# Later first seven-product pair, evenly spaced forms of x, and whole k blocks in the opening four products of a decoder step

## Chip, cores and metric

The kernel runs on one NeuronCore of a Trainium2 chip. The metric is the device time of one launch in microseconds (us), as the median over several runs.

## What is computed

One decoder layer for 264 tokens (256 of a new sequence, 8 of samples), all in float32 at the interface. Width is 2048, the inner width of each feed-forward block is 5504.

```python
def swiglu(x, wg, wu, wd):
    return (jax.nn.silu(x @ wg) * (x @ wu)) @ wd
...
        h = h + 0.5 * swiglu(rmsnorm(h, norm_ffn1[l]), ffn1_gate[l].astype(jnp.float32),
                             ffn1_up[l].astype(jnp.float32), ffn1_down[l].astype(jnp.float32))
        mix, C_f, n_f, m_f, buf = mixing_block(...)
        h = h + mix
        h = h + 0.5 * swiglu(rmsnorm(h, norm_ffn2[l]), ...)
    y = rmsnorm(h, norm_final).astype(x.dtype)
```

The change touches only the two `swiglu` parts, called layer "1" and layer "2" in the code (ffn of the first and of the second half-step).

## The kernel before, in words

**Numbers.** Every float32 weight and activation is cut into two float16 parts, hi and lo. A product of a 128x128 weight block with 264 columns of x is then three matmuls: hi with hi, hi with lo, lo with hi. The loads bring a raw float32 tile `wraw` of up to eight blocks (`fetch`, DMA issued by SP at L240); ScalarE writes `whi` (`high`, L219); VectorE writes `wlo` (`low`, L227). Six buffers of each exist and about five tiles are kept ahead (`AHEAD`). Each engine works strictly in the order in which the program emits its instructions; there is no scheduler, so the order is the one in which the Python code runs.

**Layer 1's opening.** `products4` (matmuls at L504) computes gate and up of blocks 0 and 1 together, in parts of k listed in the table `FIRST`, while x itself arrives block by block (`ahead`, DMA at L858) and is cut into its parts. Then blocks 2 and on follow as ordinary products (`product` with `three`, L286 to L288): 16 k blocks, 48 matmuls, in two tiles of eight k blocks ("chunks"). After gate of a block: product with the norm's factor, Silu; after up: product with the gate and a cut into hi and lo for the down projection. The norm's sum of squares (`square_pairs`, ScalarE L687 and VectorE L691) is formed beside this and summed over partitions by a matmul at L622 (`column_sums`), after which the outputs of blocks 0 to 2 are taken from PSUM in one go.

**Blocks by seven products.** For the blocks in `SEVEN`, gate and up are formed together as a 2x2 by 2x2 block product with seven instead of eight products, in two parts (`chunk_by_seven`, L408, c = 0 beside block j and c = 1 two blocks later): 168 matmuls of 132 columns instead of 96 of 264. This needs sums of weights, made in `prepare` (raw loads `sraw` issued by GpSimd at L330; `sa` and `sb` parts by ScalarE and VectorE; `ssum` by VectorE at L354 to L356), in eight numbered steps, one step per chunk of an ordinary product (`prepare_step`). It also needs eight forms of x (`form`: two ScalarE scalings at L658 and three GpSimd operations at L662 to L664; `form_split`: a ScalarE cut, and half a product later a VectorE cut `f` at L227). The forms use GpSimd (`side`).

**When.** `at(delta, ...)` puts a function on an agenda delta products ahead; `tick` counts a product at its start (steps of 1) and between its two chunks (0.5). The forms of x run from block 3 on (gate of block 3 is product 1), the last cut 6.5 products on. The raw loads of the first pair stand in the program just before block 3; since GpSimd has nothing ahead of them that waits, nothing in its queue holds them back in layer 1. `lag` delays each VectorE cut of weights by one tile, from block 3 on.

Of the kernel before, what the change touches and what calls it, by code (L numbers as in the profile page):

```python
# [8 lines left out]
F32 = mybir.dt.float32  # L9
# [11 lines left out]
NFB = DFF // 128  # L21
# [20 lines left out]

BRANCHING = [getattr(mybir.EngineType, e) for e in ("SP", "Activation", "PE", "DVE")]

FIRST = [(0, 1, 0, 2), (1, 1, 0, 2), (0, 1, 2, 2), (1, 1, 2, 2), (2, 1, 0, 4), (3, 1, 0, 4)]
FIRST += [(k, 2, j, 2) for k in range(4, KB, 2) for j in (0, 2)]

SEVEN = list(range(7, 22, 3)) + list(range(22, NFB, 3))  # L50
TH = T // 2


# [25 lines left out]
    return {"h": head_blocks, "c": conv_blocks, "o": lambda ob: [O + ob]}[item[0]](n)  # L79


def weight_plan(a, apart=()):


    plan = []

    def add(key, src, n, m=128):
        parts = -(-n // WK)
        cut = [n * i // parts for i in range(parts + 1)]
        for k0, k1 in zip(cut, cut[1:]):  # L90
            plan.append((key, src[:, k0:k1, :], k1 - k0, m, 1))

    def ffn(layer, first):
        gu, d = a[f"w{layer}gu"], a[f"w{layer}d"]
        for half, blocks in enumerate(HALVES):
            for j in blocks:
                if j >= first and j not in apart:
                    add((layer, "g", j), gu[j, 0], KB)
                    add((layer, "u", j), gu[j, 1], KB)
            for db in range(KB):  # L100
                b0, b1 = blocks[0], blocks[-1] + 1
                add((layer, "d", half, db), d[db][:, b0:b1, :], b1 - b0)

    four = a["w1gu"][0:2].rearrange("j g p k m -> p (j g) k m")
    for k0, nk, j0, nj in FIRST:
        plan.append(("four", four[:, j0 : j0 + nj, k0 : k0 + nk, :], nj * nk, 128, nj))
    ffn("1", 2)
    add("gates", a["wg"], KB, 64)
    for item in MIX_ORDER:
        for b in mix_blocks(item):  # L110
            add(("in", b), a["win"][b], KB)
    half = KB // 2
    for k0 in (0, half):
        for db in range(2):
            add(("out", db), a["wout"][db][:, k0 : k0 + half], half)
    for db in range(2, KB):
        add(("out", db), a["wout"][db], KB)
    ffn("2", 0)
    return plan

# [24 lines left out]
def step(ctx: ExitStack, tc: tile.TileContext, a: dict, shared, bad=None):  # L145
# [64 lines left out]

    plan = weight_plan(a, SEVEN if half_size else ())
    ready = []

    def high(dst, src, scale=1.0):
# [99 lines left out]
    def prepare(pool, layer):  # L316

        gu = a[f"w{layer}gu"]  # L320
        ks = [slice(0, 4), slice(4, 8)]
        raws = [None, None]
        steps.clear()
        step_no[0] = None

        def load(j, c):
            raws[c] = raw = pool.tile([128, 4, 4, 128], F32, tag="raw", name="sraw", bufs=2)
            for g in range(2):
                blocks = gu[j, g].rearrange("p (s k) m -> p s k m", s=2)
                queue.dma_start(raw[:, 2 * g : 2 * g + 2], blocks[:, :, ks[c], :])  # L330

        def blocks(j, c):
            if c == 0:
                formed[j, 0] = [
                    pool.tile([128, 3, 8, 128], PART, tag=f"sa{i}", name=f"sa{i}")
                    for i in range(2)
                ]
            high(formed[j, 0][0][:, :, ks[c]], raws[c][:, 0:3], sw)

        def blocks_low(j, c):  # L340
            hi, lo = formed[j, 0]
            low(lo[:, :, ks[c]], raws[c][:, 0:3], hi[:, :, ks[c]], sw)

        sums = [None]

        def all_sums(j, c):
            raw = raws[c]
            if c == 0:
                formed[j, 1] = [
                    pool.tile([128, 4, 8, 128], PART, tag=f"sb{i}", name=f"sb{i}")  # L350
                    for i in range(2)
                ]
            sums[0] = s = pool.tile([128, 4, 4, 128], F32, tag="ssum", name="ssum")
            nc.vector.tensor_tensor(s[:, 2], raw[:, 2], raw[:, 3], op=ALU.add)  # L354
            nc.vector.tensor_tensor(s[:, 3], s[:, 2], raw[:, 1], op=ALU.subtract)
            nc.vector.tensor_tensor(  # L356
                s[:, 0:2], raw[:, 0:4:2],
                s[:, 3].unsqueeze(1).to_broadcast([128, 2, 4, 128]), op=ALU.subtract,
            )
            high(formed[j, 1][0][:, :, ks[c]], s, sw)  # L360

        def sums_low(j, c):
            hi, lo = formed[j, 1]
            low(lo[:, :, ks[c]], sums[0], hi[:, :, ks[c]], sw)

        for n, j in enumerate(SEVEN):
            for s, fn, c in (
                (2, blocks, 0), (3, blocks_low, 0), (3, blocks, 1), (4, blocks_low, 1),
                (5, all_sums, 0), (6, sums_low, 0), (7, all_sums, 1), (8, sums_low, 1),
            ):  # L370
                steps.setdefault(8 * n + s - (3 if n == 0 else 0), []).append((fn, j, c))
            for c in range(2):
                s = -4 if n == 0 else 8 * n + (-2, -1)[c]
                steps.setdefault(s, []).append((load, j, c))
# [148 lines left out]
    if half_size:  # L523
        stat = const.tile([128, NSTAT], F32, name="stat")
        nc.gpsimd.memset(stat, 2.0 * SUMS[0])
        squares = const.tile([128, 6], F32, name="squares")
        twins = const.tile([128, 2, 2 * len(SEVEN)], F32, name="twins")
        twin = iter(range(2 * len(SEVEN)))

    def watch(ps, rows=None):  # L530

# [186 lines left out]
    def ffn(layer, norm, done, start=None, end=None):  # L718
        with ExitStack() as stack:
# [2 lines left out]
                tc.tile_pool(name=f"forms_{norm.tag}", bufs=1)  # L722
            )
            early = {}

            def gate_up(j, which):
                return early.pop((j, which), None) or product((layer, which, j), norm.x, range(KB))
# [47 lines left out]
                prepare(spool, layer)  # L775
            for half, blocks in enumerate(HALVES):
                act = {}
                step_end[0] = 8 * len(SEVEN) + 8

                order = []  # L780
                for i, j in enumerate(blocks):
                    if half_size and j in SEVEN:
                        order += [("seven", i, j, 0)]
                    elif half_size and j - 2 in SEVEN:
                        order += [("seven", i - 2, j - 2, 1), ("one", i, j, 0)]
                    else:
                        order += [("one", i, j, 0)]
                for kind, i, j, c in order:
                    if kind == "seven":
                        if c == 0:  # L790
                            seven[j] = [bank() for _ in range(3)]
                        chunk_by_seven(j, c, norm.x, norm.forms, seven[j])
                        if c == 1:
                            by_seven(j, i)
                        continue
                    if first and start is not None:

                        ps4 = start()
                        for n, ps in enumerate(ps4):
                            early[n // 2, "gu"[n % 2]] = ps  # L800
                        for step, pairs in ((0, (0, 1, 2)), (1, (3, 4)), (1.5, (5, 6)), (2, (7,))):
                            at(step, norm.square_pairs, fpool, pairs)
                        tick(0)
                        for which in "gu":
                            early[2, which] = product((layer, which, 2), norm.x, range(KB))
                    if half_size and j == 3:
                        for k in range(8):
                            if k:
                                at((1.5, 2.5, 3, 4, 4.5, 5.5, 6)[k - 1], norm.form_split, k - 1)
                            at((1, 1.5, 2.5, 3, 4, 4.5, 5.5, 6)[k], norm.form, k)  # L810
                        at(6.5, norm.form_split, 7)
                        for fn, *what in steps.pop(-4):
                            fn(*what)
                    if half_size and j == SEVEN[0] - 3:
                        step_no[0] = -4
                    if half_size and half == 0 and j == blocks[-1]:

                        step_end[0] = step_no[0]
                    lag[0] = half_size and j >= 3
                    pg = gate_up(j, "g")  # L820
                    if first:
                        norm.finish()
                        first = False
                    zg = t264("ta")
                    nc.vector.tensor_tensor(zg, pg, norm.r, op=ALU.mult)
                    watch(pg)
                    sg = t264("tb")
                    nc.scalar.activation(sg, zg, AF.Silu)
                    pu = gate_up(j, "u")
                    zu = t264("tc")  # L830
                    nc.vector.tensor_tensor(zu, pu, norm.r, op=ALU.mult)
                    activated(j, i, zu, sg)
                    watch(pu)
# [827 lines left out]
```

## Time and profile before

| | before |
|---|---|
| median of 3 runs | 1831.66 us (1831.6 to 1832.43) |
| profiled execution, its own time | 1831.9 us |
| its span | 1830.2 us |
| TensorE (PE) busy | 1799.4 us, 98% |
| VectorE (DVE) busy | 1400.8 us, 77% |
| ScalarE (ACT) busy | 955.9 us, 52% |
| GpSimd (POOL) busy | 248.2 us, 14% |
| HBM read and written | 366.72 and 11.78 MB, 207 GB/s over the span |

The profile is of one execution; it stands 0.24 us from the median. Times in its rows are microseconds from the start of the span. In a row of the timeline come the start, the duration, the engine, the line, the operation, output<-inputs, shapes, the count of merged instructions, and in brackets the idle time of the engine before it with what ended that. The duration of a row of n merged matmuls reaches from the first start to the last end. An engine's "q" (SPq, POOLq) is its sequencer, which issues DMAs.

### The profile page before, as it was taken

What the parts mean: (1) busy time and instruction counts of PE and PEld (TensorE: products, weight loads), DVE (VectorE), ACT (ScalarE), POOL (GpSimd) and SP (SyncE); (2) the same over time, 40 slices, a digit from 0 to 9 for tenths busy, and PEclk for the clock granted to TensorE, in tenths of its full rate; (3) what the DMA queues carried; (4) which work ended last, traced back from release to release, by engine and by line L of the source; (5) the groups of instructions that cost most, each with busy time, mean ns of one, the idle gap of its engine ahead of it and who ended that gap; (6) DMA issues with size and microseconds to landing.
All of it is one profiled execution on the core that took longest, in us unless ns stands there. A gap on an engine that the chain in (4) does not pass through costs nothing. (4 is left out here: it accounts for less than half of the span.)

```text
span 1830.2 us, 42688 instructions
## 1 busy us (share of the span) xinstructions
PE 1799.4 (98%) x17990; PEld 1590.5 (87%) x17990; DVE 1400.8 (77%) x2151; ACT 955.9 (52%) x1332; POOL 248.2 (14%) x342
## 2 busy tenths in 40 slices
PE   7999999999999999999999999999999999999997
PEld 6789988899999888888888888889988889999886
DVE  6899985569998566888887866699986559998554
ACT  6655545345554445476666644565544335555442
POOL 1410000000000112222121022321000001000120
PEclk8999999999999999999999999999999999999999
DMA  9466567646564555888877656656567546654553
GB/s 313 151 212 216 188 199 240 204 151 216 183 222 135 197 194 183 273 279 301 274 268 256 221 190 222 205 194 211 202 196 246 192 153 208 205 202 160 179 194 100
DMA packets 118647, 381.34 MB, mean 208 GB/s; under 512 B 15116, under 2 KB 24940, under 8 KB 118448
## 3 DMA queue, kind: packets, MB, share of 16 engines
q1 hardware_dynamic: 95408, 300.19, 49.6%
q0 software_dynamic: 22080, 77.91, 12.4%
q8 instruction: 142, 2.33, 0.5%
q10 hardware_dynamic: 960, 0.45, 0.1%
q14 instruction: 57, 0.47, 0.1%
HBM read 366.72 MB, written 11.78 MB: 207 GB/s over the span
## 5 line engine op out<-in xcount | busy, mean ns | idle before, releaser
L227 DVE SCALAR_TENSOR_TENSOR wlo<-wraw,whi 128x1024 f16<-128x1024 f32 (+4 forms) x598 | 684.2, 1170 | 116.1 <-ACT whi L219 112.8
L219 ACT ACTIVATE whi<-wraw 128x1024 f16<-128x1024 f32 (+4 forms) x598 | 576.0, 997 | 165.1 <-PE ps L287 141.3
L288 PE MATMUL ps<-x,wlo 128*128 128x264 f16 x1920 | 530.0, 276 | 8.4 <-DVE wlo L227 8.4
L286 PE MATMUL ps<-x,whi 128*128 128x264 f16 x1920 | 529.9, 276 | 0.1
L287 PE MATMUL ps<-x,whi 128*128 128x264 f16 x1920 | 529.9, 276 | 0.0
L288 PEld LDWEIGHTS <-wlo 128*128 128x128 f16 x4490 | 439.3, 98 | 76.4 <-DVE wlo L227 12.0
L287 PEld LDWEIGHTS <-whi 128*128 128x128 f16 x4490 | 439.3, 98 | 65.7
L286 PEld LDWEIGHTS <-whi 128*128 128x128 f16 x4490 | 439.6, 98 | 64.9 <-issue 0.6
L288 PE MATMUL ps<-a,wlo 128*128 128x264 f16 (+2 forms) x1418 | 382.7, 273 | 0.4 <-DVE wlo L227 0.4
L286 PE MATMUL ps<-a,whi 128*128 128x264 f16 (+2 forms) x1418 | 382.8, 273 | 0.0
L287 PE MATMUL ps<-a,whi 128*128 128x264 f16 (+2 forms) x1418 | 382.8, 273 | 0.0
L286 PE MATMUL ps<-xm,whi 128*128 128x264 f16 x896 | 247.3, 276 | 0.0
L288 PE MATMUL ps<-xm,wlo 128*128 128x264 f16 x896 | 247.3, 276 | 0.0
L287 PE MATMUL ps<-xm,whi 128*128 128x264 f16 x896 | 247.3, 276 | 0.0
L219 ACT ACTIVATE sb<-ssum 128x2048 f16<-128x2048 f32 x48 | 91.7, 1911 | 185.2 <-DVE ssum L356 184.9
L408 PEld LDWEIGHTS <-sb 128*128 128x128 f16 x2304 | 134.4, 98 | 0.7
L841 DVE SCALAR_TENSOR_TENSOR h<-ps,h 128x264 f32<-128x264 f32 x62 | 26.7, 431 | 126.7 <-PE ps L288 126.7
L227 DVE SCALAR_TENSOR_TENSOR sb<-ssum,sb 128x2048 f16<-128x2048 f32 x48 | 110.3, 2298 | 7.5 <-ACT sb L219 4.9
L408 PE MATMUL ps<-f,sb 128*128 128x132 f16 x1728 | 103.3, 221 | 0.0
L408 PEld LDWEIGHTS <-sa 128*128 128x128 f16 x1728 | 101.3, 98 | 0.7
L330 POOL DMA_DIRECT2D sraw<-in_w1gu x48 | 34.6, 723 | 412.3 <-issue 406.0
L330 POOL DMA_DIRECT2D sraw<-in_w2gu x48 | 34.6, 723 | 412.3 <-issue 375.9
(255 smaller groups left out, 1682.6 us busy)
## 6 DMA issues: line engine op xcount, KB each, us to landing
wraw<-in_w2gu SPq DMA_DIRECT2D x124, 512.0 KB, 4.6
wraw<-in_w1gu SPq DMA_DIRECT2D x116, 512.0 KB, 4.7
wraw<-in_win SPq DMA_DIRECT2D x112, 512.0 KB, 5.9
wraw<-in_w1d SPq DMA_DIRECT2D x80, 448.0 KB, 4.0
wraw<-in_w2d SPq DMA_DIRECT2D x80, 448.0 KB, 4.0
sraw<-in_w1gu POOLq DMA_DIRECT2D x48, 512.0 KB, 5.4
sraw<-in_w2gu POOLq DMA_DIRECT2D x48, 512.0 KB, 5.1
wraw<-in_wout SPq DMA_DIRECT2D x32, 512.0 KB, 4.8
```

Of the source, the lines that this page charges most:

```text
L219: nc.scalar.activation(dst, src, AF.Copy, scale=scale)
L227: nc.vector.scalar_tensor_tensor(dst, src, scale, hi, op0=ALU.mult, op1=ALU.subtract)
L286: nc.tensor.matmul(ps, wh, xk[:, 0, :], start=first, stop=False)
L287: nc.tensor.matmul(ps, wh, xk[:, 1, :], start=False, stop=False)
L288: nc.tensor.matmul(ps, wl, xk[:, 0, :], start=False, stop=last)
L330: queue.dma_start(raw[:, 2 * g : 2 * g + 2], blocks[:, :, ks[c], :])
L408: nc.tensor.matmul(out, w[:, f, k, :], b(k)[:, part, :], start=(k + term == 0), stop=(k == 7 and term == 2),)
L841: nc.vector.scalar_tensor_tensor(h[db], ps, 0.5 / (sw * sa[layer]), h[db], op0=ALU.mult, op1=ALU.add)
```

## The change

```diff
-FIRST = [(0, 1, 0, 2), (1, 1, 0, 2), (0, 1, 2, 2), (1, 1, 2, 2), (2, 1, 0, 4), (3, 1, 0, 4)]
+FIRST = [(k, 1, 0, 4) for k in range(4)]
...
-SEVEN = list(range(7, 22, 3)) + list(range(22, NFB, 3))
+SEVEN = {n: list(range(j, 22, 3)) + list(range(22, NFB, 3)) for n, j in (("1", 10), ("2", 7))}
...
-                        for step, pairs in ((0, (0, 1, 2)), (1, (3, 4)), (1.5, (5, 6)), (2, (7,))):
+                        for step, pairs in ((0, (0, 1)), (1, (2, 3)), (1.5, (4, 5)), (2, (6, 7))):
...
-                    if half_size and j == 3:
-                        for k in range(8):
+                    if half_size and j == (3 if start is not None else 1):
+                        room = 2 * (sevens[0] - j) - 2
+                        for k in range(9):
+                            when = 1 + int(k * room / 8 * 2) / 2
                             if k:
-                                at((1.5, 2.5, 3, 4, 4.5, 5.5, 6)[k - 1], norm.form_split, k - 1)
-                            at((1, 1.5, 2.5, 3, 4, 4.5, 5.5, 6)[k], norm.form, k)
-                        at(6.5, norm.form_split, 7)
+                                at(when, norm.form_split, k - 1)
+                            if k < 8:
+                                at(when, norm.form, k)
                         for fn, *what in steps.pop(-4):
-                            fn(*what)
-                    if half_size and j == SEVEN[0] - 3:
+                            at(2, fn, *what)
+                    if half_size and j == sevens[0] - 3:
                         step_no[0] = -4
...
-                    lag[0] = half_size and j >= 3
+                    lag[0] = half_size and j >= (3 if start is not None else 1)
```

Where the diff leaves lines out, `SEVEN` becomes `SEVEN[layer]`, and the tile `twins` gets a size to match.

In layer 1 the first block by seven products is 10 instead of 7: block 7 becomes an ordinary block, and 11 instead of 12 blocks go by seven. Layer 2 keeps its 12, the first at block 7. The forms of x run from block 3 to block 9 in layer 1 (one per 1.5 products) and from block 1 to block 6 in layer 2 (`start` is only given in layer 1; one per 1.25 products). The raw loads of the first pair go onto the agenda for the second product of that stretch. The opening four products take each of the first four k blocks as one unit of 256 KB for all four. The changed file is five lines longer at these places, so L240 there is L241, L330 is L331.

GpSimd's queue at the start of the program, before; `sraw` are the raw weights of the first block by seven products, `form_t` is the first form of x, which waits for ScalarE's `form_b`:

```order
L204 MEMSET beyond 128x256
L205 AFFINE_SELECT beyond<-beyond 128x256
L525 MEMSET stat 128x320
L330 DMA sraw<-in_w1gu 128x2x512 x4
L662 TENSOR_TENSOR form_t<-form_b 128x264
L663 TENSOR_TENSOR form_t<-form_b,form_t 128x132
L664 TENSOR_TENSOR form_t<-form_t,form_b 128x132
```

and now:

```order
L205 MEMSET beyond 128x256
L206 AFFINE_SELECT beyond<-beyond 128x256
L526 MEMSET stat 128x320
L663 TENSOR_TENSOR form_t<-form_b 128x264
L664 TENSOR_TENSOR form_t<-form_b,form_t 128x132
L665 TENSOR_TENSOR form_t<-form_t,form_b 128x132
L331 DMA sraw<-in_w1gu 128x2x512 x4
```

The four raw loads (2 MB) moved behind the first form of x, which is made at block 3.

SP's queue at the start, before; `h` are blocks of x, `wraw` the raw weights of the opening four products:

```order
L178 DMA h_80<-in_xt 128x264
L240 DMA wraw<-in_w1gu 128x2x128
L858 DMA h_80<-in_xt 128x264
L240 DMA wraw<-in_w1gu 128x2x128 x3
L858 DMA h_81<-in_xt 128x264
L240 DMA wraw<-in_w1gu 128x4x128
```

and now:

```order
L179 DMA h_80<-in_xt 128x264
L241 DMA wraw<-in_w1gu 128x4x128
L863 DMA h_80<-in_xt 128x264
L241 DMA wraw<-in_w1gu 128x4x128
L863 DMA h_81<-in_xt 128x264
L241 DMA wraw<-in_w1gu 128x4x128
```

Each k block is one load for all four products; the bytes are the same, in two loads fewer.

VectorE's order around the first block by seven products of layer 1, before; `sa`, `ssum` and `sb` are its weights, `f` a form of x, `ta` and `tc` outputs of ordinary products:

```order
L227 SCALAR_TENSOR_TENSOR f_1140<-form_t,f_1140 128x528
L227 SCALAR_TENSOR_TENSOR wlo<-wraw,whi 128x1024
L354 TENSOR_TENSOR ssum<-sraw 128x512
L355 TENSOR_TENSOR ssum<-ssum,sraw 128x512
L356 TENSOR_TENSOR ssum<-sraw,ssum 128x1024
L227 SCALAR_TENSOR_TENSOR f_1186<-form_t,f_1186 128x528
L227 SCALAR_TENSOR_TENSOR wlo<-wraw,whi 128x1024
L227 SCALAR_TENSOR_TENSOR sb_1228<-ssum,sb_1227 128x4x512
L831 TENSOR_TENSOR tc<-ps,rstd 128x264
L733 TENSOR_TENSOR tc<-tc,tb 128x264
L536 TENSOR_REDUCE stat<-ps 128x1
L227 SCALAR_TENSOR_TENSOR f_1234<-form_t,f_1234 128x528
```

and now, at the same steps, three blocks later:

```order
L228 SCALAR_TENSOR_TENSOR f_1540<-form_t,f_1540 128x528
L228 SCALAR_TENSOR_TENSOR wlo<-wraw,whi 128x1024
L355 TENSOR_TENSOR ssum<-sraw 128x512
L356 TENSOR_TENSOR ssum<-ssum,sraw 128x512
L357 TENSOR_TENSOR ssum<-sraw,ssum 128x1024
L228 SCALAR_TENSOR_TENSOR wlo<-wraw,whi 128x1024
L228 SCALAR_TENSOR_TENSOR sb_1619<-ssum,sb_1618 128x4x512
L836 TENSOR_TENSOR tc<-ps,rstd 128x264
L735 TENSOR_TENSOR tc<-tc,tb 128x264
L537 TENSOR_REDUCE stat<-ps 128x1
```

Two of the three `f` cuts between these weight operations are gone from here; they stand among the ordinary products ahead.

More of the change, by code (lines that the diff above doesn't have):

```diff
@@ L43 @@
 BRANCHING = [getattr(mybir.EngineType, e) for e in ("SP", "Activation", "PE", "DVE")]
-FIRST = [(0, 1, 0, 2), (1, 1, 0, 2), (0, 1, 2, 2), (1, 1, 2, 2), (2, 1, 0, 4), (3, 1, 0, 4)]
+FIRST = [(k, 1, 0, 4) for k in range(4)]
 FIRST += [(k, 2, j, 2) for k in range(4, KB, 2) for j in (0, 2)]
-SEVEN = list(range(7, 22, 3)) + list(range(22, NFB, 3))
+SEVEN = {n: list(range(j, 22, 3)) + list(range(22, NFB, 3)) for n, j in (("1", 10), ("2", 7))}
+PAIRS = sum(len(v) for v in SEVEN.values())
 TH = T // 2
@@ L79, in mix_blocks, with weight_plan @@
     return {"h": head_blocks, "c": conv_blocks, "o": lambda ob: [O + ob]}[item[0]](n)
-def weight_plan(a, apart=()):
+def weight_plan(a, apart=None):
     plan = []
@@ L96, in ffn @@
             for j in blocks:
-                if j >= first and j not in apart:
+                if j >= first and (apart is None or j not in apart[layer]):
                     add((layer, "g", j), gu[j, 0], KB)
@@ L208, in step @@
         )
-    plan = weight_plan(a, SEVEN if half_size else ())
+    plan = weight_plan(a, SEVEN if half_size else None)
     ready = []
@@ L364, in sums_low @@
             low(lo[:, :, ks[c]], sums[0], hi[:, :, ks[c]], sw)
-        for n, j in enumerate(SEVEN):
+        for n, j in enumerate(SEVEN[layer]):
             for s, fn, c in (
@@ L526, in step @@
         squares = const.tile([128, 6], F32, name="squares")
-        twins = const.tile([128, 2, 2 * len(SEVEN)], F32, name="twins")
-        twin = iter(range(2 * len(SEVEN)))
+        twins = const.tile([128, 2, PAIRS], F32, name="twins")
+        twin = iter(range(PAIRS))
     def watch(ps, rows=None):
@@ L724, in ffn @@
             early = {}
+            sevens = SEVEN[layer] if half_size else []
             def gate_up(j, which):
@@ L777, in ffn @@
                 act = {}
-                step_end[0] = 8 * len(SEVEN) + 8
+                step_end[0] = 8 * len(sevens) + 8
                 order = []
                 for i, j in enumerate(blocks):
-                    if half_size and j in SEVEN:
+                    if j in sevens:
                         order += [("seven", i, j, 0)]
-                    elif half_size and j - 2 in SEVEN:
+                    elif j - 2 in sevens:
                         order += [("seven", i - 2, j - 2, 1), ("one", i, j, 0)]
```

## The prediction

> **What bounds the kernel now.** The page first, for the busy engine, then PE's table of waits (who it waited for: us in total, times, longest).
>
> ```profile
> PE 1799.4 (98%) x17990; PEld 1590.5 (87%) x17990; DVE 1400.8 (77%) x2151; ACT 955.9 (52%) x1332; POOL 248.2 (14%) x342
> ...
> PE ps L504 <- ACT whi L219: 9.0, 3, 6.7
> PE ps L288 <- DVE wlo L227: 8.8, 10, 2.3
> ```
>
> PE works nearly all the time, so a gain can only come from fewer matmul cycles, a better clock or the 18 us in these two rows. L504 is the opening of layer 1, L288 any ordinary product that waits for the lo part of a weight tile. Next the timeline of the opening, all engines.
>
> ```profile
> 3.59 2.90 POOL L330 DMA_DIRECT2D sraw<-in_w1gu  x4
> 4.22 0.74 PE L504 MATMUL ps<-x,whi 128*128 128x264 f16 x4
> 9.31 0.62 PE L504 MATMUL ps<-x,whi 128*128 128x264 f16 x4 [1.38 <-ACT whi L219]
> 16.16 0.63 ACT L219 ACTIVATE whi<-wraw 128x512 f16<-128x512 f32 x1 [5.11 <-DMA wraw<-in_w1gu]
> 16.84 1.94 PE L504 MATMUL ps<-x,whi 128*128 128x264 f16 x8 [6.67 <-ACT whi L219]
> 21.09 0.61 PE L504 MATMUL ps<-x,wlo 128*128 128x264 f16 x4
> 21.54 1.06 PE L504 MATMUL ps<-x,whi 128*128 128x264 f16 x8
> 37.74 0.28 PE L286 MATMUL ps<-x,whi 128*128 128x264 f16 x1
> ```
>
> The opening lasts from 4.22 to 37.74 us, 33.5 us for 192 matmuls. At full pace one matmul follows the other after (1.06 - 0.28) / 7 = 0.112 us (0.28 is the duration of one, last row), 21.5 us for all. Of the 12.0 us above that, 9.0 are the waits. About 2.0 are a slow clock after the long one: the eight at 16.84 follow each other at (1.94 - 0.28) / 7 = 0.237 us, and 20 matmuls take from 16.84 to 21.09, 4.25 us instead of 2.24.
>
> What is late is a load, and the DMA view in short stretches says why (queue: packets, MB, share of 16 engines; stretches 3.5 to 5, 11 to 12.5 and 16 to 18 us; q1 is SP's queue, q0 GpSimd's).
>
> ```profile
> q1 hardware_dynamic: 540, 0.31, 77.1%
> ...
> q0 software_dynamic: 137, 0.50, 89.6%
> q1 hardware_dynamic: 133, 0.08, 17.1%
> ...
> DMA packets 633, 0.72 MB, mean 361 GB/s; under 512 B 44, under 2 KB 510, under 8 KB 633
> q1 hardware_dynamic: 633, 0.72, 108.4%
> ```
>
> At 11 us the raw loads for block 7, issued at 3.59, hold 90% of the DMA time, and what PE waits for gets 17%. They are four times 128x2x512 float32, 2.10 MB.
>
> The waits at L288 sit together. Busy time by stretch (PE, PEld, DVE, ACT, POOL, clock, DMA share, GB/s):
>
> ```profile
> 60.00:70.00 10.00, 8.89 (x80) 7.57 (x79) 9.97 (x14) 7.07 (x12) 6.47 (x8) 1.00 0.57 184
> 80.00:90.00 10.00, 8.89 (x77) 7.10 (x75) 8.81 (x12) 8.97 (x13) 4.77 (x5) 1.00 0.52 159
> 90.00:100.00 10.00, 6.26 (x58) 4.98 (x58) 9.90 (x9) 5.90 (x7) 6.74 (x7) 1.00 0.36 111
> 100.00:110.00 10.00, 9.30 (x114) 8.31 (x111) 9.43 (x13) 5.05 (x6) 1.44 (x2) 1.00 0.79 272
> 1200.00:1210.00 10.00, 9.66 (x112) 8.54 (x110) 9.93 (x11) 6.72 (x9) 5.09 (x5) 1.00 0.57 187
> 1210.00:1220.00 10.00, 8.89 (x91) 7.67 (x89) 9.18 (x12) 5.17 (x5) 1.45 (x2) 1.00 0.74 252
> ```
>
> PE loses 1.1 us in the 60s, 1.1 + 3.7 + 0.7 from 80 to 110 while DVE is full, and 1.4 at the same place of layer 2. So the start is bound by the DMA stream, blocks 4 to 6 by DVE, the rest by PE.
>
> **The opening.** The raw loads leave the DMA queue here, so q1 has the engines alone. In the stretch from 3.5 us it moved 0.31 MB in 1.5 us (0.21 MB/us) with 77% of them, so 0.27 at a full share. The first unit is 256 instead of 128 KB: 0.13 MB more, some 0.6 us, and a longer cut (0.63 for this size, at 16.16), so PE begins near 4.9 instead of 4.22. A k block needs 0.40 MB (weights and x), 1.5 us at the full share and 1.9 at the pace seen, against 12 matmuls of 0.112 = 1.34 us. Over the three units after the first PE waits 0.4 to 1.7 us; I take 1.2. Later pairs of k blocks need 0.79 MB, 2.2 us at 361 GB/s, below PE's 2.7. The opening then ends at 4.9 + 21.5 + 1.2 = 27.6 us, **10.1 us earlier**. The ends are 11.3 (no wait at all) and 5.9 (a stream that merely loses 2.10 MB at 0.36 MB/us and stays late). No single gap is near 6.7 us, so I count the full clock.
>
> The Trainium skill, "DMA: Bandwidth & Descriptors", section Specifications, holds 512 B enough for line rate and puts the HBM limit at about 358 GB/s; by that the sum would lose the 1.2 us of waiting. The row at 3.5 us, with packets of 574 B on average, runs below it, at 0.27 MB/us, so the row decides.
>
> **What is late next.** Behind block 2 stands the norm's sum.
>
> ```profile
> 39.66 2.76 ACT L687 ACTIVATE sq<-h 128x528 f32<-128x528 f32 x5
> 46.88 1.28 ACT L598 ACT_TABLE_LOAD   x1
> 47.49 0.43 DVE L694 TENSOR_TENSOR acc<-sq 128x264 f32<-128x264 f32 x1
> 48.54 0.61 PE L622 MATMUL ps<-acc,ones 128*128 128x264 f32 x2
> 59.77 2.88 DVE L227 SCALAR_TENSOR_TENSOR wlo<-wraw,whi 128x1024 f16<-128x1024 f32 x2 [1.24 <-ACT whi L219]
> 61.31 0.29 PE L288 MATMUL ps<-x,wlo 128*128 128x264 f16 x1 [1.11 <-DVE wlo L227]
> ```
>
> The sum was ready at 47.92, PE took it at 48.54: only 0.6 us to spare, although PE was late. Now PE ends block 2 at 27.6 + 96 x 0.112 = 38.4. Five tiles of 0.52 MB follow the opening's loads, 1.5 us each; the opening's own are in at about 24 us, the five at 31.5, cut at 32.6. Eight squares (2.76 / 5 = 0.55 each; the last product now holds two instead of one) and one more cut of 1.06 end at 38.1; the last add (twice the columns of the fold's 0.43) and the fold end near 39.4. PE waits about 1 us (0.9 in the sum), and ACT then does two cuts (2.0) and the table load (1.28) that used to lie under PE's work, so the outputs of blocks 0 to 2, and behind them the tile of block 4, come up to 1.5 us later. Sum 2.4 us lost; 0 if the stream runs a little faster. I take **1.6 lost**. The wait of 1.11 at 61.31 belongs to the same chain and stays.
>
> **Blocks 3 to 9.** DVE's prices:
>
> ```profile
> 87.09 1.75 DVE L227 SCALAR_TENSOR_TENSOR sa<-sraw,sa 128x1536 f16<-128x1536 f32 x1
> 95.35 1.48 DVE L227 SCALAR_TENSOR_TENSOR wlo<-wraw,whi 128x1024 f16<-128x1024 f32 x1
> 99.22 0.42 DVE L831 TENSOR_TENSOR tc<-ps,rstd 128x264 f32<-128x264 f32 x1
> 100.03 0.16 DVE L536 TENSOR_REDUCE stat<-ps 128x1 f32<-128x16 f32 x1
> 100.11 0.70 DVE L227 SCALAR_TENSOR_TENSOR f<-form_t,f 128x528 f16<-128x528 f32 x1
> 100.73 1.22 DVE L227 SCALAR_TENSOR_TENSOR wlo<-wraw,whi 128x1024 f16<-128x1024 f32 x1
> 101.86 0.68 DVE L354 TENSOR_TENSOR ssum<-sraw 128x512 f32<-128x512 f32 x1
> 102.58 0.69 DVE L355 TENSOR_TENSOR ssum<-ssum,sraw 128x512 f32<-128x512 f32 x1
> 103.31 1.22 DVE L356 TENSOR_TENSOR ssum<-sraw,ssum 128x1024 f32<-128x1024 f32 x1
> 1214.20 2.29 DVE L227 SCALAR_TENSOR_TENSOR sb<-ssum,sb 128x2048 f16<-128x2048 f32 x1 [0.50 <-ACT sb L219]
> ```
>
> A product takes PE 5.38 us and DVE two `wlo` and 1.0 us of output work (per block of two products four operations like the 0.42 and two like the 0.16), 3.5 us. The first pair's weights cost 2 x (1.75 + 2.59 + 2.29) = 13.3 us. Before, blocks 4 to 6 held all that, seven forms at about 0.75 and twelve `wlo` at 1.35 (they take 1.48 while POOL makes a form): 16.2 + 6.0 + 13.3 + 5.2 = 40.7 us against 32.3 of PE, 8.4 over. In layer 1 the tile lead was nil at the start (the wait at 61.31), and 1.1 + 3.7 + 0.7 = 5.5 us came up as stalls; in layer 2 the same 8.4 met a full lead and only 0.3 + 1.1 = 1.4 came up, so a lead covers about 7.
>
> Now the products from block 4 to 7 (eight) want 3.5 + 0.5 for the forms against 5.38, so the lead is rebuilt. Blocks 8 and 9 hold 8 x 1.22 + 4.0 + 13.3 + two forms 1.4 = 28.5 against 21.5: 7.0 over, which the lead just covers. I take 0.3 of the 5.5 as left: **5.2 gained**, bounds 5.5 and 1.5 (the lead half there). A moved form keeps its seven operations; between its POOL steps ACT now does more weight cuts, so it waits for POOL less. The raw loads pass the first form in POOL's queue and occupy it for 2.9 us, while the second form follows the first by 1.5 products, eight us; they collide with a steady stream at 159 to 184 GB/s, below the 361 it can do, and five tiles are ahead.
>
> **Block 7 of layer 1.** By seven it is 168 matmuls at the pace of the first row, less one matmul's own 0.22 us from the second, (4.30 - 0.22) / 71 = 0.0575 us:
>
> ```profile
> 116.98 4.30 PE L408 MATMUL ps<-f,sb 128*128 128x132 f16 x72
> ...
> L408 PE MATMUL ps<-f,sb 128*128 128x132 f16 x1728 | 103.3, 221 | 0.0
> ```
>
> That is 9.66 us; ordinary it is 96 x 0.112 = 10.75. PE is on the path: **1.1 lost**. DVE and ACT get less to do there, the loads are equal in bytes.
>
> **Layer 2.** Forms start two blocks earlier, in a stretch where PE lost nothing; three of seven leave blocks 4 to 6. Of the 1.4 us I count **1.2 gained**, bounds 1.4 and a loss of 0.5, should the earlier `lag` (one tile less lead from block 1) make a tile late.
>
> **Sum.** -10.1 + 1.6 - 5.2 + 1.1 - 1.2 = -13.8 us. The profiled execution took 1831.9 us (span 1830.2), 0.24 above the median; taken from the median of 1831.66, 1817.9 us.
>
> **The rivals.**
> - *The stream stays the bound of the opening.* Then it gains 5.9 only: -5.9 + 1.6 - 5.2 + 1.1 - 1.2 = -9.6, 1822.1 us. For it: q1 reached only 0.21 MB/us at first. Against: from 16 us on it outruns PE. Chance 0.17.
> - *DVE stalls PE before block 10 as before block 7.* 4.0 of the 5.5 and layer 2's 1.4 stay: -10.1 + 1.6 - 1.5 + 1.1 = -8.9, 1822.8 us. For it: 7.0 over against a cover of 7. Against: layer 2 bore 8.4. Chance 0.10.
> - *Small packets go at the full stream rate* (the page named above). No waits, the sum in time: -11.3 - 5.5 + 1.1 - 1.4 = -17.1, 1814.6 us. Chance 0.09.
> - *Slower: the clock.* If the short waits of the opening add up to a half clock all through it, it takes 192 x 0.237 = 45.5 us from 4.9, ends at 50.4, 12.7 later: +12.7 - 5.2 + 1.1 - 1.2 = +7.4, 1839.1 us. It decides when gaps are long enough to drop the clock: 6.67 us was, 1.38 at 9.31 was not ((0.62 - 0.28) / 3 = 0.113 after it). Chance 0.03, and 0.02 that half of the opening is so, which nets about nothing (+6.4 - 5.3 = +1.1). The Trainium skill, "TensorE: Matmul & The Clock Gate", Part 1, puts the drop at an idle window of about 3.4 us; both gaps agree with that.
>
> That the loads don't move can be left aside: they stand behind an operation that waits for ACT's form.
>
> **Chances.** Forecast 0.59, then 0.17, 0.10, 0.09, 0.03, 0.02. Something under 0.2% (3.7 us) can't be told from no change: faster 0.95, same 0.02, slower 0.03. The range, 1813 to 1823, takes in the forecast with its bounds and the three faster rivals.
>
> **What would show it.** Right: `sraw` loads behind the first form near 53 us; first block-2 matmul at L287 (L286 before) near 27.6; no PE gap over 2 us at L505 and clock 1.0 after 9 us; a wait of 1 to 2.6 us before block 4; PE dense to block 10; 11 + 12 blocks at L409. Wrong: block 2 beginning after 31 us; a wait at the sum of squares of over 2 us; DVE at 9.9 of 10 with PE under 9 in blocks 8 and 9; a new wait in layer 2's blocks 1 to 3.

## The result, and the profile after

| | before | changed |
|---|---|---|
| median of 6 runs each | 1831.76 us (1831.0 to 1833.98) | 1816.49 us (1816.18 to 1817.92) |
| profiled execution, its own time | 1831.9 us | 1816.65 us |
| its span | 1830.2 us | 1814.9 us |

The ratio is 0.9917, 95% interval 0.9904 to 0.993: 15.3 us less, where 13.8 us less was forecast.

The page's first row and the waits of TensorE (PE) in the changed kernel (who waited for whom: us in total, times, longest):

```profile
PE 1797.8 (99%) x17918; PEld 1591.0 (88%) x17918; DVE 1388.2 (76%) x2141; ACT 953.1 (53%) x1329; POOL 237.2 (13%) x338
...
PE ps L962 <- DVE ok L956: 2.0, 1, 2.0
PE ps L289 <- DVE wlo L228: 1.5, 3, 1.1
PE idle L192 <- DVE ones L182: 1.1, 1, 1.1
PE ps L623 <- DVE acc L695: 1.1, 1, 1.1
PE ps L505 <- ACT whi L220: 0.6, 1, 0.6
PE ps L287 <- ACT whi L220: 0.2, 1, 0.2
```

The 9.0 us of the opening (now L505) have become 0.6, and that wait stands ahead of the first unit. The 8.8 us at ordinary products (L289) have become 1.5, and a new row stands there: the sum of squares, 1.1 us. The opening's timeline, and GpSimd's first form with the raw loads behind it:

```profile
5.00 1.94 PE L505 MATMUL ps<-x,whi 128*128 128x264 f16 x8 [0.59 <-ACT whi L220]
6.74 0.77 PE L505 MATMUL ps<-x,wlo 128*128 128x264 f16 x4
7.65 1.07 PE L505 MATMUL ps<-x,whi 128*128 128x264 f16 x8
27.91 0.28 PE L287 MATMUL ps<-x,whi 128*128 128x264 f16 x1
...
50.74 0.75 POOL L663 TENSOR_TENSOR form_t<-form_b 128x264 f32<-128x264 f32 x1 [47.10 <-ACT form_b L659]
...
53.38 2.90 POOL L331 DMA_DIRECT2D sraw<-in_w1gu  x4
```

PE starts at 5.00 and is at block 2 at 27.91 instead of 37.74. Its first 12 matmuls take 2.65 us instead of the 1.34 of the full pace; behind them it waits for nothing until block 2. The raw loads start at 53.38 instead of 3.59. The DMA view of the same 11 to 12.5 us that the prediction quoted now holds SP's queue only (packets, MB, share of 16 engines):

```profile
DMA packets 482, 0.54 MB, mean 363 GB/s; under 512 B 34, under 2 KB 404, under 8 KB 482
q1 hardware_dynamic: 482, 0.54, 108.2%
```

That is 0.54 MB of wanted data where there were 0.08. Then the timeline of the chain of the norm's sum, and of the longer of the two waits before block 4 (the other, at L287, is 0.2 us):

```profile
38.76 1.28 ACT L599 ACT_TABLE_LOAD   x1
39.36 0.43 DVE L695 TENSOR_TENSOR acc<-sq 128x264 f32<-128x264 f32 x1
39.94 0.68 PE L623 MATMUL ps<-acc,ones 128*128 128x264 f32 x2 [1.06 <-DVE acc L695]
53.17 0.29 PE L289 MATMUL ps<-x,wlo 128*128 128x264 f16 x1 [1.11 <-DVE wlo L228]
```

The sum is ready at 39.79, and PE has waited 1.06 us for it. The stretches (PE, PEld, DVE, ACT, POOL, clock, DMA share, GB/s) in which the first pair's weights are made, in layer 1 (blocks 8 and 9) and in layer 2:

```profile
100.00:110.00 10.00, 10.00 (x92) 8.70 (x90) 9.93 (x12) 4.79 (x8) 4.42 (x5) 1.00 0.45 152
1190.00:1200.00 10.00, 10.00 (x126) 9.24 (x125) 9.71 (x12) 6.30 (x7) 1.45 (x2) 1.00 0.72 248
```

VectorE is as full as before (9.93 of 10), and PE loses nothing beside it: the tiles it needs were cut earlier.

To add the stages up, the first chunk by seven products of block 10 serves as a mark in both traces, before and after:

```profile
131.92 2.92 PE L408 MATMUL ps<-x,sa 128*128 128x132 f16 x48
```

```profile
117.76 2.92 PE L409 MATMUL ps<-x,sa 128*128 128x132 f16 x48
```

The opening ends 9.8 us earlier, from there to block 10 it is 94.2 against 89.8 us (4.3 gained, the dearer block 7 included), together 14.2. The first product of layer 2 begins at 1130.5 against 1116.3, the same 14.2 us earlier. The last matmul of its ordinary gate and up products (L286, now L287) starts at 1702.3 against 1686.3, 16.0 us earlier, so layer 2 gave 1.8. Behind that, the last stores took 0.7 back (15.3 between the spans).

### The profile page after: what moved, and what is told of

The parts are those of the page before. It is cut to its first block, busy times and chain, and to the rows that moved or that the text cites. A ratio compares the mean times of both kernels' runs of the same rounds, so it can differ in the third digit from the quotient of the medians.

```text
span 1814.9 us, 42526 instructions
## 1 busy us (share of the span) xinstructions
PE 1797.8 (99%) x17918; PEld 1591.0 (88%) x17918; DVE 1388.2 (76%) x2141; ACT 953.1 (53%) x1329; POOL 237.2 (13%) x338
## 5 line engine op out<-in xcount | busy, mean ns | idle before, releaser
L228 DVE SCALAR_TENSOR_TENSOR wlo<-wraw,whi 128x1024 f16<-128x1024 f32 (+2 forms) x600 | 688.2, 1172 | 103.5 <-ACT whi L220 102.9
L220 ACT ACTIVATE whi<-wraw 128x1024 f16<-128x1024 f32 (+2 forms) x600 | 580.0, 1000 | 160.6 <-PE ps L288 140.7
L289 PE MATMUL ps<-x,wlo 128*128 128x264 f16 x1952 | 538.8, 276 | 1.1 <-DVE wlo L228 1.1
L287 PE MATMUL ps<-x,whi 128*128 128x264 f16 x1952 | 538.8, 276 | 0.2 <-ACT whi L220 0.2
L288 PE MATMUL ps<-x,whi 128*128 128x264 f16 x1952 | 538.8, 276 | 0.0
L289 PEld LDWEIGHTS <-wlo 128*128 128x128 f16 x4522 | 442.5, 98 | 67.4 <-DVE wlo L228 2.4
L287 PEld LDWEIGHTS <-whi 128*128 128x128 f16 x4522 | 442.7, 98 | 65.6 <-issue 0.6
L289 PE MATMUL ps<-a,wlo 128*128 128x264 f16 (+2 forms) x1418 | 382.7, 273 | 0.4 <-DVE wlo L228 0.4
L287 PE MATMUL ps<-a,whi 128*128 128x264 f16 (+2 forms) x1418 | 382.8, 273 | 0.0
L287 PE MATMUL ps<-xm,whi 128*128 128x264 f16 x896 | 247.3, 276 | 0.0
L289 PE MATMUL ps<-xm,wlo 128*128 128x264 f16 x896 | 247.3, 276 | 0.0
L409 PEld LDWEIGHTS <-sb 128*128 128x128 f16 x2208 | 128.8, 98 | 0.7
L228 DVE SCALAR_TENSOR_TENSOR sb<-ssum,sb 128x2048 f16<-128x2048 f32 x46 | 105.2, 2288 | 8.0 <-ACT sb L220 5.6
L409 PE MATMUL ps<-f,sb 128*128 128x132 f16 x1656 | 99.0, 221 | 0.0
L409 PEld LDWEIGHTS <-sa 128*128 128x128 f16 x1656 | 97.1, 98 | 0.7
L331 POOL DMA_DIRECT2D sraw<-in_w2gu x48 | 34.6, 723 | 420.7 <-issue 371.5
L228 DVE SCALAR_TENSOR_TENSOR sa<-sraw,sa 128x1536 f16<-128x1536 f32 x46 | 81.8, 1778 | 3.1
```

The costliest lines, as they stand in the source:

```text
L220: nc.scalar.activation(dst, src, AF.Copy, scale=scale)
L228: nc.vector.scalar_tensor_tensor(dst, src, scale, hi, op0=ALU.mult, op1=ALU.subtract)
L287: nc.tensor.matmul(ps, wh, xk[:, 0, :], start=first, stop=False)
L288: nc.tensor.matmul(ps, wh, xk[:, 1, :], start=False, stop=False)
L289: nc.tensor.matmul(ps, wl, xk[:, 0, :], start=False, stop=last)
L409: nc.tensor.matmul(out, w[:, f, k, :], b(k)[:, part, :], start=(k + term == 0), stop=(k == 7 and term == 2),)
```

## The experiments

All are given with the median of their runs; 1831.76 and 1816.49 us are the two kernels above, and 1832.2 to 1833.1 us the kernel before as it ran beside the experiments. That kernel's median moved by up to 1.4 us between the series of runs, so a smaller difference between kernels of different series is not resolved by medians; there the traces have to decide.

**The raw loads at the start again**, layer 1 only:

```diff
-                            at(2, fn, *what)
+                            fn(*what) if start is not None else at(2, fn, *what)
```

> The changed kernel, but layer 1's first four raw loads stand in GpSimd's queue ahead of the first form again, so that they start at 3.6 us. Theory (their 2.1 MB held up the opening): the opening ends at 36 to 38 us instead of 27.8, with a gap of PE of over 5 us and a half clock behind it; the 1.1 us wait for the sum of squares goes; 1824 to 1826 us. Rival (whole k blocks as units made the opening shorter): within 1.5 us of the 1816.5 of the changed kernel, opening below 30 us.

1823.32 us (1822.54 to 1823.83). PE's waits up to 120 us:

```profile
PE ps L505 <- ACT whi L220: 6.3, 2, 5.6
...
PE ps L289 <- DVE wlo L228: 0.7, 1, 0.7
```

and block 2's start in its timeline:

```profile
37.45 0.28 PE L287 MATMUL ps<-x,whi 128*128 128x264 f16 x1
```

The opening is back at 37.45, all of the 9.8 us but 0.3: the loads made it long. The whole costs 6.8 us, less than the 7.5 to 9.5 expected, because with PE late the waits at the sum and before block 4 go (0.7 left of 1.1 + 1.3).

**The old table of the opening**, on the changed kernel, and later once more on the kernel with early squares (below):

```diff
-FIRST = [(k, 1, 0, 4) for k in range(4)]
+FIRST = [(0, 1, 0, 2), (1, 1, 0, 2), (0, 1, 2, 2), (1, 1, 2, 2), (2, 1, 0, 4), (3, 1, 0, 4)]
```

> The changed kernel with the old table for the opening four products (k blocks 0 and 1 in two halves each). Theory (the units matter little once the raw loads are gone): PE begins 0.6 us earlier on a smaller first load, two more loads cost some of it, the opening ends between 27 and 29 us, 1815.5 to 1818 us. Rival (the units carry the gain of the opening): it ends after 31 us, 1820 us or more.

> The kernel with early squares, with the old table for the opening four products. Theory (the units are worth less than 1 us): 1813.7 to 1814.7 us, the opening ends between 27.7 and 28.7 us. Rival (the units carry part of the gain): 1815.5 us or more.

1816.84 us (1815.84 to 1818.22), and 1814.21 (1813.49 to 1815.27) where the base has 1813.76. Block 2 begins at 28.55 and 29.29 us, 0.6 and 1.6 later than in the bases' profiles. The second of these starts is beyond the 28.7 us expected, while both times are as the theory had them. The units are worth between nothing and some 1.5 us; the runs don't resolve more. They are not what shortened the opening.

**The forms packed as before**, pair of layer 1 still at 10:

```diff
-                    if half_size and j == (3 if start is not None else 1):
+                    if half_size and j == 3:
...
-                            when = 1 + int(k * room / 8 * 2) / 2
...
+                                at((1.5, 2.5, 3, 4, 4.5, 5.5, 6)[k - 1], norm.form_split, k - 1)
+                            at((1, 1.5, 2.5, 3, 4, 4.5, 5.5, 6)[k], norm.form, k)
...
-                    lag[0] = half_size and j >= (3 if start is not None else 1)
+                    lag[0] = half_size and j >= 3
```

> The changed kernel with the old timetable of the forms (from block 3, the last cut 6.5 products on, in both layers) and the delay of the lo cuts from block 3. Theory (in layer 1 the later pair alone would do, the spacing matters in layer 2, where the pair stays at block 7): no new wait of PE in blocks 3 to 10 of layer 1, the 1.4 us of layer 2 come back, 1817.5 to 1818.5 us. Rival (the spacing removed layer 1's stalls): 3 to 5.5 us of waits in layer 1, 1820.5 to 1823.5 us.

1822.95 us (1821.64 to 1824.79). By its time that is the rival's range, but not by its reason. The trace, of the slowest of the four executions, has 2.4 us of waits in blocks 4 to 9, less than the rival's 3 to 5.5 and more than the theory's none, 2.3 in layer 2, and something else: a longer wait for the sum, then a half clock (second fence, stretches as above).

```profile
41.76 0.68 PE L623 MATMUL ps<-acc,ones 128*128 128x264 f32 x2 [3.06 <-DVE acc L695]
```

```profile
42.00:44.00 2.00, 2.00 (x11) 1.36 (x11) 2.00 (x3) 1.50 (x2) 0.00 (x0) 0.63 0.11 20
44.00:46.00 2.00, 2.00 (x12) 1.39 (x10) 1.90 (x6) 0.60 (x2) 0.00 (x0) 0.52 0.84 268
46.00:48.00 2.00, 2.00 (x20) 1.74 (x18) 1.41 (x7) 0.54 (x3) 0.00 (x0) 1.00 0.69 221
```

Nothing of the edit stands ahead of that wait. ACT begins the last weight cut ahead of the squares at 32.40 us here and at 30.58 in the changed kernel, and from 20 to 42 us the cuts waited 2.1 us for loads and 1.9 us for VectorE and PE here, 2.3 us for loads alone there. Where the opening ends early and the squares stand behind it, the wait is 0.3 to 3.1 us in these traces, so this run could not price the spacing; a steadier base was needed.

**Early squares.** Four of the eight squares go into the opening, and each form comes half a product later at the first:

```diff
-                        for step, pairs in ((0, (0, 1)), (1, (2, 3)), (1.5, (4, 5)), (2, (6, 7))):
+                        for step, pairs in ((0, (4,)), (1, (5,)), (1.5, (6,)), (2, (7,))):
...
-                            when = 1 + int(k * room / 8 * 2) / 2
+                            when = 1.5 + int(k * (room - 0.5) / 8 * 2) / 2
...
+            if k0 >= 8:
+                n1.square_pairs(n1.fpool, (k0 // 2 - 4,))
```

> The changed kernel with four of the eight squares of the norm (and their adds) put into the opening four products, behind the cuts of k blocks 8, 10, 12 and 14, and each form of x at the first at half a product later, so that the cut of block 4's first weight tile stands ahead of the first form on ScalarE. Theory (what is late after the opening is the chain of squares, then the chain of outputs): the wait for the sum of squares (1.1 us) and the two at block 4 (1.3 us) go, 1814 to 1815 us. Rival (the four squares make the cuts of the opening late): new waits in the opening of 1 us or more, 1816 us or more.

1813.76 us (1813.7 to 1813.87), ratio to the kernel before 0.9893 (0.9876 to 0.9909), just under the range expected. The sum is ready in time, and of the waits before block 4 one of 0.5 us is left. VectorE's fold and PE's sum:

```profile
37.99 0.43 DVE L695 TENSOR_TENSOR acc<-sq 128x264 f32<-128x264 f32 x1
...
38.57 0.68 PE L623 MATMUL ps<-acc,ones 128*128 128x264 f32 x2
```

It beats both kernels. Its four runs lie within 0.2 us where the changed kernel's spread over 1.7. That would fit if the wait for the sum made the spread, but the kernels below that are built on this one spread over 0.8 to 1.8 us with hardly any such wait, so that is not shown.

**Packed forms in one layer at a time**, on that base; `packed` is the old timetable:

```diff
+                            when = packed[k] if start is not None else when
```

For layer 2 the condition is `start is None`, and there the forms and the delay of the lo cuts begin at block 3 again. The old timetable begins at product 1, the base's at product 1.5.

> The kernel with early squares (1813.76 us, runs within 0.2 us of each other, so the base for prices from here on), with the old timetable of the forms in layer 1 alone. Theory as it stands after the packed run (spacing has its own part in layer 1, because packed forms come when the lead is nil): 1.5 to 2.5 us of PE waits in blocks 4 to 9, 1815.0 to 1816.3 us. Rival (the later pair alone is enough): no waits beyond the 0.5 us at block 4, 1813.6 to 1814.3 us.

> The kernel with early squares, with the old timetable of the forms (from block 3) and of the delay of the lo cuts in layer 2 alone. Theory (spacing is all that changed there): PE waits of 1.4 to 2.3 us before layer 2's first block by seven come back, 1815.2 to 1816.2 us. Rival (layer 2's stalls came from elsewhere): 1813.6 to 1814.3 us.

1817.91 us (1817.46 to 1818.21) with layer 1 packed, 1816.85 (1815.93 to 1817.77) with layer 2: 4.2 and 3.1 us, both above the ranges expected. PE's waits at ordinary products over the whole kernel, on the base:

```profile
PE ps L289 <- DVE wlo L228: 0.9, 3, 0.5
```

with layer 1 packed:

```profile
PE ps L289 <- DVE wlo L228: 3.9, 7, 1.1
...
PE ps L287 <- ACT whi L220: 0.3, 1, 0.3
```

and with layer 2 packed:

```profile
PE ps L289 <- DVE wlo L228: 3.4, 6, 1.2
```

That is 3.3 us more in five more waits, and 2.5 us more in three. A matmul lasts 0.28 us, but in the flow one starts every 0.11 us, and a wait counts only from the end of the one before. So each wait costs 0.17 us beside its idle time: 3.3 + 0.85 = 4.2 and 2.5 + 0.5 = 3.0, close to the 4.2 and 3.1 of the medians.

Not all of it is the packing. From 45 to 60 us, before block 4, the kernel with layer 1 packed has

```profile
PE ps L289 <- DVE wlo L228: 1.1, 1, 1.1
PE ps L287 <- ACT whi L220: 0.3, 1, 0.3
```

where the base has one wait of 0.5 us. The changed kernel, spaced but begun at product 1, has nearly the same two (1.1 and 0.2), so they come with the first form half a product earlier and cost about 1.0 us. Four waits of 2.3 us behind them belong to the packing: with 4 x 0.17, 3.0 us. In layer 2, two waits of 2.3 us stand before the first block by seven; counted from layer 2's first product to the last matmul of its ordinary ones, the packing costs 2.6 us there, and the remaining 0.5 arose ahead of layer 2, where this edit changes nothing.

Whom ScalarE (ACT) waited for from 52 to 100 us in layer 1 (blocks 4 to 8), packed:

```profile
ACT f L220 <- POOL form_t L665: 11.0, 7, 3.0
```

and not packed, on the base:

```profile
ACT a L220 <- DVE tc L735: 5.6, 4, 1.9
ACT tb L833 <- DVE ta L830: 5.4, 3, 2.5
ACT f L220 <- POOL form_t L665: 0.9, 2, 0.8
```

A packed form is cut half a product or a product after it is begun. ACT reaches the cut before GpSimd is done, waits, and the weight cuts queued behind it come late, and VectorE's with them. One such chain in the timeline of the packed kernel:

```profile
62.28 0.64 ACT L220 ACTIVATE f<-form_t 128x528 f16<-128x528 f32 x1 [2.97 <-POOL form_t L665]
...
64.71 1.47 DVE L228 SCALAR_TENSOR_TENSOR wlo<-wraw,whi 128x1024 f16<-128x1024 f32 x1 [1.05 <-ACT whi L220]
...
66.24 0.29 PE L289 MATMUL ps<-x,wlo 128*128 128x264 f16 x1 [0.86 <-DVE wlo L228]
```

The busy time of the packed kernel shows that VectorE's capacity is not what PE waits for there:

```profile
60.00:70.00 10.00, 9.13 (x82) 7.71 (x81) 6.97 (x9) 6.06 (x10) 6.07 (x9) 1.00 1.00 369
80.00:90.00 10.00, 9.09 (x80) 7.44 (x79) 7.89 (x12) 7.25 (x11) 2.53 (x3) 1.00 0.54 173
```

VectorE has 2 to 3 us of 10 to spare in the very stretches in which PE loses 0.9. The kernel before has the same row in its blocks 4 to 6 (57 to 105 us), the changed one has none (49 to 118 us):

```profile
ACT f L219 <- POOL form_t L664: 8.9, 6, 2.1
```

**The pair at 7**, all else as changed; the rule then gives nearly the packed timetable, since eight products are left for it (the last cut comes at 7 instead of 6.5):

```diff
-SEVEN = {... for n, j in (("1", 10), ("2", 7))}
+SEVEN = {... for n, j in (("1", 7), ("2", 7))}
```

> The changed kernel with layer 1's first block by seven products at 7 again; the forms then go into blocks 3 to 6 by the same rule, one per 0.75 product, and the raw loads stay late. Theory (VectorE has 8.4 us too much in blocks 4 to 6 and no lead there): 5.5 us of PE waits return before block 7, 1.1 us are saved by the twelfth block by seven, 1820 to 1822 us. Rival (the stalls came from the late opening, so the lead is now full as in layer 2): 1.4 us of waits, 1816 to 1817.5 us.

1824.0 us (1823.66 to 1825.05), 7.5 us more and above the range. Waits between 45 and 110 us:

```profile
PE ps L289 <- DVE wlo L228: 6.7, 6, 2.3
PE ps L409 <- DVE f L228: 1.4, 1, 1.4
```

The second row is new: the first chunk by seven has its weights but not the last form, which is cut half a product later than in the kernel before. So the early pair with packed forms loses some 8.6 us (7.5, and 1.1 that a twelfth block by seven saves), of which about 3 come from packing alone.

**Only the loads moved**, on the kernel before:

```diff
-                            fn(*what)
+                            at(2, fn, *what)
```

> The kernel before with one edit: the raw loads of the first pair go onto the agenda for the second product of the forms' stretch, in both layers; units, timetable and blocks by seven as before. Theory (one part of the change, the opening, is worth about 8 us by itself, and the stalls of VectorE in blocks 4 to 6 stay): opening ends near 28 us instead of 37.7, 5.5 to 7.6 us of PE waits before block 7 and 1.4 to 2.3 in layer 2; 1823 to 1826 us. Rival (the stalls were a consequence of the late opening and shrink with it): 1818 to 1820 us.

1826.97 us (1826.47 to 1827.9), 1 us above the range. The opening ends at 28.47, but only some 5 us of the 9.3 arrive. The wait for the sum is 2.6 us with a half clock behind it (first the timeline, then a stretch as above):

```profile
42.01 0.95 PE L622 MATMUL ps<-acc,ones 128*128 128x264 f32 x2 [2.57 <-DVE acc L694]
```

```profile
44.00:46.00 2.00, 2.00 (x13) 1.40 (x11) 1.90 (x7) 0.86 (x2) 0.00 (x0) 0.57 0.91 279
```

And 6.7 us of waits stay from 45 to 115 us. The rival fails: the stalls were not a consequence of the late opening.

**The pair at 13**, on the changed kernel and on the base with early squares:

```diff
-SEVEN = {... for n, j in (("1", 10), ("2", 7))}
+SEVEN = {... for n, j in (("1", 13), ("2", 7))}
```

> The changed kernel with layer 1's first block by seven at 13 instead of 10, so 10 instead of 11 blocks by seven there; the forms go over blocks 3 to 12. Theory (TensorE is the bound behind block 4, an ordinary block costs 10.75 us and one by seven 9.66): 1.1 us more than the changed kernel, 1817.6 us, no new waits; the first chunk by seven starts 30.8 us later or within 1 us of that. Rival (VectorE is still the hidden bound in blocks 8 to 12, and one pair fewer relieves it): no more than 1816.5 us.

> The kernel with early squares, with layer 1's first block by seven at 13 instead of 10. Theory (an ordinary block costs TensorE 1.1 us more than one by seven and nothing else changes): 1814.6 to 1815.1 us. Rival (VectorE still costs something in blocks 8 and 9, which goes with the pair): 1813.2 to 1814.2 us.

1816.86 us (1815.55 to 1817.58) and 1814.06 (1813.94 to 1815.59). By the medians that is 0.3 to 0.4 us more, less than the series resolve, and less than the 1.1 expected. In the traces of the second pair of kernels, VectorE's last six operations:

```profile
1803.96 2.10 DVE L904 TENSOR_TENSOR h<-h,rstd 128x256 f32<-128x256 f32 x6
```

```profile
1802.78 2.10 DVE L904 TENSOR_TENSOR h<-h,rstd 128x256 f32<-128x256 f32 x6
```

The kernel with the pair at 13 (first row) computes 1.2 us longer, though its opening ended 0.3 us earlier. Of these 1.5 us some 0.4 are a wait at the sum (0.2 and the 0.17 of a wait), which leaves the 1.1 that the pace of the matmuls says. Its last stores then ended 6.3 us after that work instead of 7.3, so the spans differ by 0.2. Why the stores' time differs was not tried. The second time lies in the rival's range, but neither trace has a wait of PE in blocks 5 to 12, so VectorE costs nothing there that a later pair could save.

**A longer warm-up**, more idle matmuls ahead of the first unit:

```diff
-WARM = 29
+WARM = 40
```

> The changed kernel with 40 instead of 29 idle matmuls ahead of the first weights, which end near 5.0 us instead of 4.4. Theory (the first unit runs at half clock in the changed kernel because TensorE's warm-up stops before the larger first unit arrives): the first eight matmuls follow each other at 0.112 instead of 0.237 us in the profile, about 1 us is saved, 1815 to 1816 us. Rival (the clock comes up at a time of its own, whatever is issued just before): first unit unchanged in some executions, 1816 to 1817 us.

1816.44 us (1815.66 to 1817.02), no difference, in the rival's range. The first unit ran at full clock in this trace, but so it did in some of those with 29. The one with the pair at 13 on the changed kernel shows what a fast first unit meets:

```profile
4.90 1.07 PE L505 MATMUL ps<-x,whi 128*128 128x264 f16 x8 [0.69 <-ACT whi L220]
...
7.14 1.07 PE L505 MATMUL ps<-x,whi 128*128 128x264 f16 x8 [0.71 <-ACT whi L220]
```

PE waits 0.7 us for the second unit, and with 40 idle matmuls it waits 0.4 and 0.5 us behind the first. Block 2 begins at 27.5 and 28.2 us, at 27.9 in the changed kernel with its slow first unit. Those waits end with a cut, and from 4 to 13 us ACT waited 1.9 and 2.7 us for weight loads in these two traces. So a slow first unit costs next to nothing here: a fast one has to wait for the loads.

## Why the prediction was right, and where not

- *The opening, 10.1 us less from 27.6.* It was 9.8, and block 2 began at 27.91. The cause is shown: the loads alone bring 9.5 us of the opening back. The make-up was off: where 1.2 us of waits over three units were counted at full clock, no wait came behind the first unit, but its 12 matmuls ran at about half pace and lost 1.3 us. That the two are of one size is not only luck: in the traces of this table with a fast first unit 0.7 to 1.0 us of waits for the next loads stand behind it, and block 2 begins at 27.5 to 28.2.
- *What is late next, 1.6 lost.* The named chain it was: sum ready at 39.79 (39.4 forecast), wait 1.06 (0.9 forecast), but before block 4 only 0.2 on top of the old 1.1, where up to 1.5 were allowed. That is 1.3 us idle in two waits, 1.6 with the 0.17 of each; the sum alone made PE wait 0.3 to 3.1 us in the other traces with an early opening and late squares. That a gap here can cost a half clock as well was not foreseen.
- *Blocks 3 to 9, 5.2 gained.* With 1.1 for block 7 and 1.6 for the chain taken out, the marks give 4.3 + 1.1 + 1.6 = 7.0. The term was too small because it took the idle time for the loss: each of the five waits costs 0.17 us beside its idle time, and 0.4 us of the last one, behind 110 us, were left out.
- *Its reason was half right.* "So the start is bound by the DMA stream, blocks 4 to 6 by DVE" is the step that fell short: VectorE's sum of 40.7 us against 32.3 did not name ACT's wait for GpSimd, 8.9 us in order ahead of the weight cuts, which packing brings back (3.0 us) with VectorE at 7 to 8 of 10. The rest, 4.0 of the 7.0 us here and 5.6 of the 8.6 with the pair put back to 7, appears only where the pair's weights meet the packed forms; how much of that is VectorE's load and how much the chain was not separated. The prediction mentioned that ACT would wait for POOL less, and gave it no price. That the change spread the forms as well as moving the pair is why the term came out in spite of this; as far as the prediction goes, that is luck.
- *Block 7, 1.1 lost.* Agrees with the traces (1.1 with the wait at the sum taken out); the medians don't resolve it.
- *Layer 2, 1.2 gained.* 1.8 by the marks, and 2.6 us to lose by packing on the base with early squares. The row of ACT's wait for GpSimd is there too: 9.7 us before. The earlier delay of the lo cuts made no wait in the changed kernel.
- *The rivals.* The stream did not stay the bound. Stalls between block 4 and block 10: none. Small packets at full rate: no, a fast first unit still waits 0.4 us or more for the next loads. A half clock did come, for 12 matmuls, not for 192. The price of half an opening at half pace was mis-added: 4.9 + 96 x 0.237 + 96 x 0.112 = 38.4 us is 0.7 later than before, not 6.4, so that rival stood at -4.6 us, not at +1.1.
- *The sum.* -9.8 + 1.6 - 7.0 + 1.1 - 1.8, and 0.7 of the stores at the end, which no term had, make -15.2. What came out larger than forecast lies in blocks 3 to 9 and layer 2; the stores took part of it back.

## What to carry to other kernels

A transfer that nothing holds back starts when its queue reaches it, not where the program names it; loads for later work belong behind something that waits. Before calling an engine the bound, look at whom the engine ahead of it waits for in order: spreading a chain over three engines can free more than its busy time. And when PE is made earlier, the next chain in line sets the gain, and a gap in it can cost the clock too.

## What the runs showed of the hardware

- Beside large packets, small ones get little: the raw loads held 89.6% of the DMA time at 11 us, SP's queue 17.1%. The two moved nearly the same number of packets in these 1.5 us (137 and 133), but 0.50 and 0.08 MB. Alone SP's queue had all and moved 363 GB/s.
- A gap of PE of 3.06 us was followed by about 3.3 us at half pace (clock 0.63 and 0.52), one of 2.57 us by about 3.7 (clock 0.57); gaps of 1.06 to 1.4 us were not. The Trainium skill, "TensorE: Matmul & The Clock Gate", Part 1, puts the drop at an idle window of about 3.4 us that runs on its own; here gaps shorter than that were enough.
- After the warm-up of 29 the first unit ran at 0.237 us per matmul in some executions and at 0.11 to 0.13 in others, with gaps of 0.4 to 0.7 us ahead of it in the one kind and 0.5 to 0.7 in the other.
- The clock in the rows read 1.00 from 4 to 8 us in the changed kernel while its matmuls followed each other at 0.237 us; the pace of the matmuls is the surer reading.
